# First modulation in two halves, and other orders of work in the first stage

## The chip, the cores and the metric

The kernel is one layer of a hybrid block and runs on one core of one Trainium2 chip. The core's engines are TensorE (PE; its weight loads are PEld), VectorE (DVE, in the code V), ScalarE (ACT, in the code S) and GpSimd (POOL, in the code G); SyncE (SP) issues most DMA loads. The metric is the device time in microseconds of one execution; a kernel's time is the median of its runs.

## The reference

The layer has two parts. The first makes a modulation from a conditioning vector, normalises and modulates 512 latent and 256 context tokens of width 1024, projects them, mixes one half by a two-dimensional DFT and the other by two gated linear recurrences (forward and backward), and projects back. The second retrieves 16 of 16384 experts per head and token.

```python
mod_x = silu(c) @ w_mod + b_mod          # six vectors of 1024: sh1, sc1, g1, sh2, sc2, g2
mod_c = silu(c_ctx) @ w_mod + b_mod      # of these only sh1, sc1 matter
hx = rmsnorm(x, norm1_g) * (1 + sc1_x) + sh1_x
hc = rmsnorm(ctx, norm1_g) * (1 + sc1_c) + sh1_c
fx, ux, gx = split(hx @ w_in);  uc = (hc @ w_in)[u columns]
ux, uc = dwconv(ux), dwconv(uc)
for d, rev in ((0, False), (1, True)):   # r, i: sigmoid gates of the convolved u
    a = exp(-8 * r * softplus(-lam))     # decay
    h = scan(a, sqrt(1 - a * a) * i * u) # context first, then latent
rx = (h_forward + h_backward) * gelu(gx)
x = x + g1 * (concat(rmsnorm(fourier_mix(fx)), rmsnorm(rx)) @ w_out)
h2 = rmsnorm(x, norm2_g) * (1 + sc2) + sh2
x = x + g2 * peer_ffn(h2);  out = rmsnorm(x, final_norm_g)
```

## The kernel before

Everything lies transposed: 128 partitions hold 128 channels, the free axis holds tokens (256 of the context, `C`, then 512 latent, `T`), and eight tiles `d` make the width of 1024. Products in high precision are three matmuls each (`mm3`, lines 131 to 134): every operand is split in a high part (ACT copies it, line 70) and a low part (V, or G where the call says so, subtracts, line 123); `split_w` does this for 1024 columns of a weight.

Weights come in 1 MB blocks through `load` (line 115) into rotating buffers of the pool `raws`: two of the tag `raw`, two of `rawU`. A load waits until a buffer of its tag is free. The loads up to `graw` (`wgate`) are issued by SP in the order of the code (`in_order(first_load, ...)`); later ones where the framework's planner puts them. PE, ACT and V run the first stage in the order of the code, in two stretches that `in_order(start, ...)` fixes; POOL's order is the planner's.

The modulation is 24 blocks of `w_mod`, eight for each third. `mod_mm(n)` (line 217) multiplies block `n` by the conditioning; `mod_out(m)` copies the sum, transposes it with four small matmuls (line 225) and adds the bias (line 229). The first third gives shift and scale of the first norm, for latent and context (`mods`, `modc`). The order of the first stage is: sums of squares of `x` (line 247) and its reciprocal root (`rsqrt`, lines 151 to 154), blocks 0 to 2, sums of squares of the context, blocks 3 to 7, `mod_out(0)`, `A1` (the scale, line 262). Then for each `d` come `hx_norm` (V multiplies by scale and root, line 267; ACT adds the shift and rounds to the high part), `hx_low` (V makes the low part, line 272) and `u_mm`, the projection to the first half of `u`, with the two splits of `wu0` and the decay rates (`decay_rates`, 26 small operations on V, lines 294 to 309) in between.

The second stretch starts with `u_evac` and `conv` and goes on in the order written out in the middle of the code: `gates(k)` (two directions, two gates, each with one context and one latent product into one of five PSUM buffers, freed by ACT's sigmoid), `decays` (lines 396, 397), `scans` (lines 404 to 413; the sum of the two directions is line 413), `gate_branch`, the Fourier products `f_mm`, the DFT over positions `dft_seq` and over channels `dft_head`, `rec_out`, and the output projection `out_mm` in eight parts, each followed by `out_add`. `mod_cols(w)` issues one more block of the modulation and multiplies the one before. The second norm's sums of squares are `x2_sums`; `rstd2` is its root. Then `h2` (lines 705 to 707) and the routing loop over eight heads, whose query weights `wq` are split with the low part on G.

Of the kernel before, what the change touches and what calls it, by code (L numbers as in the profile page):

```python
# [51 lines left out]
def build(tc, xT, ctxT, c2t, vecs, wm, wu, wf, wg, wgate, wo, wq, keys, u, v, urow, vrow,  # L52
# [158 lines left out]
    def mod_mm(n):  # L211
        m, d = n // 8, n % 8
        if d == 0:
            modp[m] = pst("pm")
        t = rawm.pop(n)
        for j in range(4):
            PE.matmul(modp[m][32 * j:32 * j + 32], cc32[:, d], t[:, j * 512:(j + 1) * 512],  # L217
                      start=(d == 0), stop=(d == ND - 1))

    def mod_out(m):  # L220
        sb = bt(F32, 512)
        act(sb, modp[m], AF.Copy)
# [4 lines left out]
        for z, mm in enumerate((mods, modc)[:2 if m == 0 else 1]):
            sl = slice(16 * m, 16 * m + 16)
            V.tensor_tensor(mm[:, sl].rearrange("p (j b) -> p j b", j=4), pv[:, z],
                            vec[:, V_BMOD + 16 * m:V_BMOD + 16 * m + 16].rearrange("p (j b) -> p j b", j=4), op=ALU.add)  # L230
# [52 lines left out]
    hx_norm(0)  # L283
    wpu = [split_w(rawu[0], 0)]
    hx_norm(1)
    hx_low(0)
    wpu.append(split_w(rawu[0], 1))
    hx_norm(2)
    hx_low(1)
    u_mm(pss0, wpu, 0)  # L290
    u_mm(pss0, wpu, 1)

    def decay_rates():
        V.tensor_scalar(s_, e_, 2.0, None, op0=ALU.add)
        V.reciprocal(s_, s_)
        V.tensor_tensor(s_, s_, e_, op=ALU.mult)
        V.tensor_tensor(q_, s_, s_, op=ALU.mult)
        V.memset(sp, 1.0 / 17)
        yield
        for n in (15, 13, 11, 9, 7, 5, 3, 1):  # L300
            V.tensor_tensor(sp, sp, q_, op=ALU.mult)
            V.tensor_scalar(sp, sp, 1.0 / n, None, op0=ALU.add)
            if n in (11, 5):
                yield
        V.tensor_tensor(sp, sp, s_, op=ALU.mult)
        V.tensor_scalar(e_, lam, -1.0, 0.0, op0=ALU.mult, op1=ALU.max)
        V.scalar_tensor_tensor(sp, sp, 2.0, e_, op0=ALU.mult, op1=ALU.add)
        V.tensor_scalar(z8, sp, 8.0, None, op0=ALU.mult)
        V.tensor_scalar(n8, sp, -8.0, None, op0=ALU.mult)

    decay = decay_rates()
    for d in range(3, ND):
        hx_norm(d)
        hx_low(d - 1)
        next(decay, None)
        u_mm(pss0, wpu, d - 1)
    hx_low(ND - 1)
    u_mm(pss0, wpu, ND - 1)
    for _ in decay:
        pass  # L320
# [78 lines left out]
    def scans(ks):  # L399
        for k in ks:  # L400
            for dr in range(2):
# [6 lines left out]
                else:  # L408
# [865 lines left out]
```

## Time and profile before

| | before |
|---|---|
| median of 3 runs | 1479.88 us (1477.38 to 1479.92) |
| profiled execution | 1475.7 us, its span 1473.9 us |
| PE busy | 1390.8 us (94%) |
| DVE busy | 1234.7 us (84%) |
| ACT busy | 614.4 us (42%) |
| POOL busy | 689.6 us (47%) |
| mean granted TensorE clock | 0.973 |
| DMA | 420.61 MB, mean 285 GB/s |

The profile is one execution. Busy time is an average over stages with different limits; the first stage, up to about 270 us, is where the change lies. In a timeline each row has start and length in microseconds, the engine, the line, the operation, what it writes and reads with the shape, the number of merged instructions, and in brackets how long the engine had been idle before it and what ended that. The granted clock is a share of 2.4 GHz: 1.00 is that, 0.50 is 1.2 GHz.

### The profile page before, as it was taken

The numbers are of one execution on the slowest core, as the hardware profiler recorded it, in microseconds if no ns is written. First come the engines' busy times: TensorE is split into PE (matmuls) and PEld (weight loads), VectorE is DVE, ScalarE is ACT, GpSimd is POOL, SyncE is SP. The second block draws the span as 40 slices with busy tenths as digits, with TensorE's granted clock in tenths as the row PEclk, the third lists the DMA queues.
The fourth block names the chain that finished last, engine by engine and source line by source line (L and its number), as shares of the span: only waits on it lengthen the run. The fifth ranks groups of instructions, "written<-read, shape, count | busy, mean of one in ns | idle before, by whom it ended". The sixth has DMA issues, their size and how long they took to land.

```text
span 1473.9 us, 22547 instructions
## 1 busy us (share of the span) xinstructions
PE 1390.8 (94%) x8561; PEld 1285.8 (87%) x8561; DVE 1234.7 (84%) x2178; ACT 614.4 (42%) x880; POOL 689.6 (47%) x466
## 2 busy tenths in 40 slices
PE   5798888999989999999999999998999999899995
PEld 2676655888878999999999999998999999899995
DVE  2867874699987999388989898998898999999973
ACT  3468642534333556443333433333343343343341
POOL 0035255466430000255767656675675765645412
PEclk9899999999999999999999999999999999999998
DMA  9324347232225999999999998999999999999911
GB/s 369 125 80 177 143 172 259 90 128 84 90 77 173 317 305 300 366 342 374 371 367 405 356 409 331 400 369 376 393 378 389 385 375 405 411 415 415 394 45 57
DMA packets 130189, 420.61 MB, mean 285 GB/s; under 512 B 10400, under 2 KB 59808, under 8 KB 106016
## 3 DMA queue, kind: packets, MB, share of 16 engines
q1 hardware_dynamic: 83520, 251.03, 45.7%
q0 software_dynamic: 46560, 168.14, 29.6%
q8 instruction: 67, 1.10, 0.3%
q14 instruction: 42, 0.34, 0.1%
HBM read 385.41 MB, written 33.69 MB: 284 GB/s over the span
## 4 chain that ended last, share of the span: by engine, by line
PE 57%; DVE 12%; DMA 11%; issue 9%; POOL 6%; ACT 3%; SPq 0%; DVEq 0%; POOLq 0%; ACTq 0%
PE ps_ps L132 8%; PE ps_ps L133 8%; PE ps_ps L134 8%; PE ps_pa L132 8%; PE ps_pa L133 8%; PE ps_pa L134 8%; POOL row L1065 6%; DMA row<-vrow,eidx 4%; DMA row<-urow,eidx 4%; DVE wlo L123 2%; DVE oacc L1086 1%; ACT b L70 1%; PE ps_pm L217 1%; ACT whi L70 1%; DVE row L1072 1%
## 5 line engine op out<-in xcount | busy, mean ns | idle before, releaser
L70 ACT ACTIVATE whi<-raw 128x1024 fp32r<-128x1024 f32 x296 | 312.6, 1059 | 602.0 <-PE ps_pa L133 296.8
L123 DVE TENSOR_TENSOR wlo<-raw,whi 128x1024 fp32r<-128x1024 f32 x264 | 328.3, 1246 | 48.3 <-ACT whi L70 46.5
L132 PE MATMUL ps_pa<-h2h,whi 128*128 128x352 f32 x1024 | 336.6, 329 | 4.9 <-ACT act L70 4.9
L133 PE MATMUL ps_pa<-h2l,whi 128*128 128x352 f32 x1024 | 336.0, 328 | 0.0
L134 PE MATMUL ps_pa<-h2h,wlo 128*128 128x352 f32 x1024 | 335.8, 328 | 0.2 <-DVE wlo L123 0.2
L1065 POOL DMA_INDIRECT row<-vrow,eidx x128 | 191.4, 1495 | 133.0 <-DVE oacc L1086 96.7
L1065 POOL DMA_INDIRECT row<-urow,eidx x128 | 198.3, 1549 | 113.2 <-DVE row L1072 57.5
L133 PE MATMUL ps_ps<-wl,whi 128*128 128x352 f32 x640 | 206.8, 323 | 0.0
L134 PE MATMUL ps_ps<-wh,wlo 128*128 128x352 f32 x640 | 206.6, 323 | 0.0
L132 PE MATMUL ps_ps<-wh,whi 128*128 128x352 f32 x640 | 206.4, 323 | 0.0
L132 PEld LDWEIGHTS ps_pa<-h2h,whi 128*128 128x128 f32 x1024 | 195.1, 191 | 6.9 <-ACT act L70 5.6
L134 PEld LDWEIGHTS ps_pa<-h2h,wlo 128*128 128x128 f32 x1024 | 194.6, 190 | 1.3 <-DVE wlo L123 0.4
L133 PEld LDWEIGHTS ps_pa<-h2l,whi 128*128 128x128 f32 x1024 | 194.8, 190 | 0.9
L1072 DVE SCALAR_TENSOR_TENSOR row<-row,hrow 128x1024 f32<-128x1024 f32 x128 | 153.8, 1219 | 32.9 <-DMA row<-urow,eidx 32.5
L1086 DVE SCALAR_TENSOR_TENSOR oacc<-row,gw,oacc 128x1024 f32<-128x1024 f32 x127 | 162.5, 1280 | 11.3 <-DMA row<-vrow,eidx 10.6
L134 PEld LDWEIGHTS ps_ps<-wh,wlo 128*128 128x128 f32 x640 | 120.2, 188 | 0.2 <-DVE wlo L123 0.2
L133 PEld LDWEIGHTS ps_ps<-wl,whi 128*128 128x128 f32 x640 | 120.2, 188 | 0.0
L132 PEld LDWEIGHTS ps_ps<-wh,whi 128*128 128x128 f32 x640 | 120.2, 188 | 0.0
L123 POOL TENSOR_TENSOR wlo<-raw,whi 128x1024 fp32r<-128x1024 f32 x32 | 77.2, 2414 | 91.8 <-ACT whi L70 63.9
L133 PE MATMUL ps_pa<-wl,whi 128*128 128x352 f32 x256 | 82.7, 323 | 0.0
L134 PE MATMUL ps_pa<-wh,wlo 128*128 128x352 f32 x256 | 82.6, 323 | 0.0
L132 PE MATMUL ps_pa<-wh,whi 128*128 128x352 f32 x256 | 82.5, 322 | 0.0
(296 smaller groups left out, 2610.3 us busy)
## 6 DMA issues: line engine op xcount, KB each, us to landing
raw<-u SPq DMA_DIRECT2D x64, 1024.0 KB, 7.5
raw<-v SPq DMA_DIRECT2D x64, 1024.0 KB, 7.9
raw<-wm SPq DMA_DIRECT2D x24, 1024.0 KB, 5.9
Gd<-stg SPq DMA_DIRECT2D x22, 1024.0 KB, 7.6
gt<-Gd SPq DMA_DIRECT2D x16, 1408.0 KB, 11.5
raw<-wq SPq DMA_DIRECT2D x8, 1024.0 KB, 5.2
Ad<-act SPq DMA_DIRECT2D x10, 704.0 KB
act<-Ad SPq DMA_DIRECT2D x10, 704.0 KB
```

Of the source, the lines that this page charges most:

```text
L70: return S.activation(o, i, f, **kw)
L123: lo_ins[0] = (lo_eng or V).tensor_tensor(dst[1], src, dst[0].bitcast(F32), op=ALU.subtract).ins
L132: PE.matmul(ps, a[0], b[0], start=start, stop=False)
L133: PE.matmul(ps, a[0], b[1], start=False, stop=False)
L134: PE.matmul(ps, a[1], b[0], start=False, stop=stop)
L217: PE.matmul(modp[m][32 * j:32 * j + 32], cc32[:, d], t[:, j * 512:(j + 1) * 512], start=(d == 0), stop=(d == ND - 1))
L1065: G.indirect_dma_start(out=t, out_offset=None, in_=tab, in_offset=bass.IndirectOffsetOnAxis(ap=e[:, s:s + 1], axis=0))
L1072: ins = V.scalar_tensor_tensor(t, t, 1.0, hr, op0=ALU.mult, op1=ALU.mult, accum_out=dt[:, s:s + 1])
L1086: ins = V.scalar_tensor_tensor(o, t, g[:, s:s + 1], o, op0=ALU.mult, op1=ALU.add)
```

## The change

The first third of the modulation is laid out anew on the host: blocks 0 to 3 hold the columns of the scale, blocks 4 to 7 those of the shift, each block two tiles `d` of 1024 columns. Each half has its own sum (`mod_first`), and the sum over the two tiles is part of the transposes. The scale is applied to all `d` of `x` before the context's squares are summed; the shifts follow after. `wu0` is loaded ahead of blocks 4 to 7, with its two splits between blocks 5 and 6; the decay rates stand right after the root of `x`. The sum of the two scan directions goes from G to V. The second half of the gate weights (`gp[1]`) is split before the first decays; the first two parts of `w_out` are split after the first DFT head, and a modulation block stands before that head. In the output projection the sums of squares follow the second part instead of the first; block 23 and `mod_out(2)` stand in the eighth part, and the query weights of head 0 are loaded and split (on V) within the loop.

```diff
-    for n in range(4, 8):
-        mod_load(n, ("", "U")[n % 2])
-    rawu = {0: load(wu[0], cuts=2)}
+    rawu = {0: load(wu[0], cuts=2)}
+    for n in range(4, 8):
+        mod_load(n, ("U", "")[n % 2])
     def mod_mm(n):
+        t = rawm.pop(n)
+        if n < 8:
+            m, first, final = -1 - n // 4, n % 4 == 0, n % 4 == 3
+            ds = [2 * (n % 4) + j // 2 for j in range(4)]
+        else:
+            m, first, final = n // 8, n % 8 == 0, n % 8 == 7
+            ds = [n % 8] * 4
+        if first:
             modp[m] = pst("pm")
         for j in range(4):
-            PE.matmul(modp[m][32 * j:32 * j + 32], cc32[:, d], t[:, j * 512:(j + 1) * 512],
-                      start=(d == 0), stop=(d == ND - 1))
+            PE.matmul(modp[m][32 * j:32 * j + 32], cc32[:, ds[j]], t[:, j * 512:(j + 1) * 512],
+                      start=first, stop=final)
+    def mod_first(z):
+        sb = bt(F32, 512)
+        act(sb, modp[-1 - z], AF.Copy)
+        pT = pst("pa", 32)
+        for b in range(4):
+            PE.matmul(pT[:, 4 * b:4 * b + 4], sb[:, b * P:(b + 1) * P], vec[:, V_SEL2:V_SEL2 + 4], start=True, stop=True)
+        pv = pT[:, :16].rearrange("p (b j z) -> p z j b", b=4, j=2)
+        o = 8 - 8 * z
+        for k, mm in enumerate((mods, modc)):
+            V.tensor_tensor(mm[:, o:o + 8].rearrange("p (j b) -> p j b", j=2), pv[:, k],
+                            vec[:, V_BMOD + o:V_BMOD + o + 8].rearrange("p (j b) -> p j b", j=2), op=ALU.add)
...
     rsqrt(rstd[:, sx], m[:, sx], ssx, 1024)
-    for n in range(3):
+    V.tensor_scalar(s_, e_, 2.0, None, op0=ALU.add)
+    V.reciprocal(s_, s_)
...
+    V.tensor_scalar(n8, sp, -8.0, None, op0=ALU.mult)
+    for n in range(4):
         mod_mm(n)
-    mean_squares([xn[d][:, sc] for d in range(ND)], C, ssc, range(ND))
-    rsqrt(rstd[:, sc], m[:, sc], ssc, 1024)
-    for n in range(3, 8):
-        mod_mm(n)
-    mod_out(0)
+    mod_first(0)
     A1 = cpool.tile([P, 2, ND], F32, name="A1")
...
+    for d in range(ND):
+        hx_norm(d, 0, x2[d], sx)
+    mean_squares([xn[d][:, sc] for d in range(ND)], C, ssc, range(ND))
+    rsqrt(rstd[:, sc], m[:, sc], ssc, 1024)
+    for d in range(ND):
+        hx_norm(d, 1, xn[d][:, sc], sc)
+    mod_mm(4)
+    mod_mm(5)
+    wpu = [split_w(rawu[0], h) for h in range(2)]
+    mod_mm(6)
+    mod_mm(7)
+    mod_first(1)
...
+    for d in range(ND):
+        hx_high(d)
+        hx_low(d)
+        u_mm(pss0, wpu, d)
...
-                    G.tensor_tensor(hsum[-1][:, C:], hsum[-1][:, C:], r[:, C:], op=ALU.add)
+                    V.tensor_tensor(hsum[-1][:, C:], hsum[-1][:, C:], r[:, C:], op=ALU.add)
...
     y_split(3)
+    gp[1] = split_w(graw, 1)
     decays([0, 1])
     gate_branch(1)
     gate_weights(3)
-    gp[1] = split_w(graw, 1)
     scans([0, 1])
...
     scans([3])
-    wpo = {k: out_weights(k) for k in range(2)}
...
+    mod_cols(7, "U")
     Y0 = dft_head(0, ab0)
-    mod_cols(7, "U")
+    wpo = {k: out_weights(k) for k in range(2)}
     ab0 = dft_seq(2)
...
+    psk = {}
     for k in range(8):
-        pss = out_mm(k, wpo[k], Ys if k < 4 else mr)
-        if k == 0:
+        psk[k] = out_mm(k, wpo[k], Ys if k < 4 else mr)
+        if k == 1:
             ssf, ssr = pst("pa"), pst("pa")
...
-        out_add(k, pss, rF if k < 4 else None)
+            out_add(0, psk[0], rF)
+        if k:
+            out_add(k, psk[k], rF if k < 4 else None)
...
         if k < 7:
             mod_cols(9 + k, "U")
+        if k == 5:
+            raw0 = load(wq[0])
+        if k == 7:
+            mod_mm(23)
+            mod_out(2)
+        if k == 6:
+            wpq = [split_w(raw0, p, V) for p in range(2)]
     x2_sums(3)
     rsqrt(rstd2, bt(F32, 512), ss2[0], 1024)
-    mod_mm(23)
-    mod_out(2)
...
-            wp = split_w(raw, p, G)
+            wp = split_w(raw, p, G) if h else wpq[p]
```

## Rows read from the trace of the kernel before

**Rows 1.** Stretches: length, busy us (x) of PE, PEld, DVE, ACT, POOL, clock, DMA share, GB/s.
```profile
32.80:49.87 17.07, 10.39 (x34) 7.22 (x35) 9.72 (x20) 7.03 (x11) 0.00 (x0) 0.50 0.72 283
...
67.35:112.57 45.22, 44.46 (x232) 35.39 (x230) 31.72 (x43) 27.04 (x40) 15.00 (x8) 1.00 0.25 94
115.57:121.55 5.98, 5.21 (x15) 4.04 (x15) 5.19 (x6) 5.79 (x7) 0.00 (x0) 0.50 0.76 284
122.36:168.76 46.40, 44.97 (x234) 34.49 (x234) 40.44 (x31) 35.33 (x49) 23.16 (x12) 1.00 0.44 161
168.76:186.71 17.95, 13.56 (x97) 10.61 (x96) 11.58 (x19) 6.71 (x16) 6.14 (x4) 0.90 0.39 136
271.08:1473.90 1202.82, 1164.94 (x7471) 1126.10 (x7470) 1057.10 (x1935) 473.96 (x670) 597.48 (x411) 0.98 0.82 308
```
**Rows 2.** Timeline of PE: modulation blocks, transposes, and the start and end of `u_mm`.
```profile
30.64 1.07 PE L217 MATMUL ps_pm<-raw,cc 128*32 128x512 f32 x8 [1.42 <-DMA raw<-wm]
33.13 1.94 PE L217 MATMUL ps_pm<-raw,cc 128*32 128x512 f32 x8 [1.43 <-DMA raw<-wm]
35.79 1.88 PE L225 MATMUL ps_pa<-vec,b 128*128 128x8 f32 x8 [0.72 <-ACT b L70]
41.10 0.58 PE L132 MATMUL ps_ps<-b,whi 128*128 128x256 f32 x1 [3.43 <-ACT whi L70]
...
65.05 0.27 PE L132 MATMUL ps_ps<-b,whi 128*128 128x256 f32 x1
...
67.14 0.28 PE L132 MATMUL ps_ps<-b,whi 128*128 128x256 f32 x1
```
**Rows 3.** Timeline of SP: two issues of loads.
```profile
31.77 0.33 SPq L115 DMA_DIRECT2D raw<-wgate  x1
...
94.86 0.33 SPq L115 DMA_DIRECT2D raw<-wm  x1
```
**Rows 4.** The chain that ended last: start, length, what; a load from issue to use.
```profile
129.63 4.80 DMA raw<-wf
```
**Rows 5.** Timeline of DVE: a norm of 512 columns, a weight split, a decay rate's step.
```profile
42.62 0.74 DVE L267 SCALAR_TENSOR_TENSOR b<-x,A,b 128x512 f32<-128x512 f32 x1
...
45.10 1.22 DVE L123 TENSOR_TENSOR wlo<-raw,whi 128x1024 fp32r<-128x1024 f32 x1 [0.68 <-ACT whi L70]
...
60.54 0.17 DVE L305 TENSOR_TENSOR sp<-sp,s__152 128x8 f32<-128x8 f32 x1
```
**Rows 6.** Timeline of PE at `gates(2)`: its first matmul and the one after the stop.
```profile
115.57 0.58 PE L132 MATMUL ps_ps<-b,whi 128*128 128x256 f32 x1 [3.00 <-ACT whi L70]
...
122.36 0.50 PE L132 MATMUL ps_ps<-b,whi 128*128 128x512 f32 x1 [0.90 <-ACT b L70]
```
**Rows 7.** Timeline of ACT between `decays` and `scans`.
```profile
113.53 1.99 ACT L70 ACTIVATE whi<-raw 128x1024 fp32r<-128x1024 f32 x2
```
**Rows 8.** Timelines of DVE and PE around the Fourier head.
```profile
157.09 3.43 DVE L123 TENSOR_TENSOR wlo<-raw,whi 128x1024 fp32r<-128x1024 f32 x2
...
168.38 3.40 DVE L123 TENSOR_TENSOR wlo<-raw,whi 128x1024 fp32r<-128x1024 f32 x2
...
172.44 0.39 PE L133 MATMUL ps_pa<-b,c_sb 128*128 128x258 f32 x1 [3.68 <-DVE b L123]
```
**Rows 9.** Timelines of PE and DVE in the output projection.
```profile
196.32 1.78 PE L653 MATMUL ps_pa<-b,ones 128*128 128x512 f32 x2 [2.93 <-POOL b L567]
...
204.43 1.40 DVE L628 SCALAR_TENSOR_TENSOR b<-ps_ps,mods,b 128x512 f32<-128x512 f32 x2
...
217.26 3.47 DVE L558 SCALAR_TENSOR_TENSOR b<-b,vec 128x512 fp32r<-128x512 f32 x2
...
219.86 1.06 PE L217 MATMUL ps_pm<-raw,cc 128*32 128x512 f32 x8
```
**Rows 10.** Timelines of ACT and DVE before `h2`.
```profile
248.03 1.99 ACT L70 ACTIVATE whi<-raw 128x1024 fp32r<-128x1024 f32 x2
...
252.09 2.71 DVE L153 TENSOR_TENSOR b<-b,rstd 128x512 f32<-128x512 f32 x1
```

More of the change, by code (lines that the diff above doesn't have):

```diff
@@ L37 @@
 NG = P // JG
-V_BMOD, V_N1, V_N2, V_FN, V_CW, V_CB, V_BA, V_BX, V_LAM, V_FG, V_LG, V_SEL = (
-    0, 48, 56, 64, 72, 88, 92, 100, 108, 116, 120, 124)
-NV = 132
+V_BMOD, V_N1, V_N2, V_FN, V_CW, V_CB, V_BA, V_BX, V_LAM, V_FG, V_LG, V_SEL, V_SEL2 = (
+    0, 48, 56, 64, 72, 88, 92, 100, 108, 116, 120, 124, 132)
+NV = 136
 NBUF = 35
@@ L226, in mod_out @@
         pv = pT.rearrange("p (b j z) -> p z j b", b=4, j=4)
[L227 to L230, printed above, removed]
+        sl = slice(16 * m, 16 * m + 16)
+        V.tensor_tensor(mods[:, sl].rearrange("p (j b) -> p j b", j=4), pv[:, 0],
+                        vec[:, V_BMOD + 16 * m:V_BMOD + 16 * m + 16].rearrange("p (j b) -> p j b", j=4), op=ALU.add)
     hx = []
@@ L252, in build @@
     rsqrt(rstd[:, sx], m[:, sx], ssx, 1024)
-    for n in range(3):
-        mod_mm(n)
-    mean_squares([xn[d][:, sc] for d in range(ND)], C, ssc, range(ND))
-    rsqrt(rstd[:, sc], m[:, sc], ssc, 1024)
-    for n in range(3, 8):
-        mod_mm(n)
-    mod_out(0)
+    V.tensor_scalar(s_, e_, 2.0, None, op0=ALU.add)
+    V.reciprocal(s_, s_)
+    V.tensor_tensor(s_, s_, e_, op=ALU.mult)
+    V.tensor_tensor(q_, s_, s_, op=ALU.mult)
+    V.memset(sp, 1.0 / 17)
+    for n in (15, 13, 11, 9, 7, 5, 3, 1):
+        V.tensor_tensor(sp, sp, q_, op=ALU.mult)
+        V.tensor_scalar(sp, sp, 1.0 / n, None, op0=ALU.add)
+    V.tensor_tensor(sp, sp, s_, op=ALU.mult)
+    V.tensor_scalar(e_, lam, -1.0, 0.0, op0=ALU.mult, op1=ALU.max)
+    V.scalar_tensor_tensor(sp, sp, 2.0, e_, op0=ALU.mult, op1=ALU.add)
+    V.tensor_scalar(z8, sp, 8.0, None, op0=ALU.mult)
+    V.tensor_scalar(n8, sp, -8.0, None, op0=ALU.mult)
+    for n in range(4):
+        mod_mm(n)
+    mod_first(0)
     A1 = cpool.tile([P, 2, ND], F32, name="A1")
@@ L262, in build, with hx_norm, hx_high @@
         V.scalar_tensor_tensor(A1[:, z], mm[:, 8:16], 1.0, vec[:, V_N1:V_N1 + 8], op0=ALU.add, op1=ALU.mult)
-    def hx_norm(d):
+    def hx_norm(d, z, src, sl):
+        V.scalar_tensor_tensor(xn[d][:, sl], src, A1[:, z, d:d + 1], rstd[:, sl], op0=ALU.mult, op1=ALU.mult)
+    for d in range(ND):
[10 more added lines that the diff above has]
+    mod_first(1)
+    parts = ((sc, modc), (sx, mods))
+    def hx_high(d):
         hx.append(bt2(L))
-        for z, src, sl, mm in ((1, xn[d][:, sc], sc, modc), (0, x2[d], sx, mods)):
-            V.scalar_tensor_tensor(xn[d][:, sl], src, A1[:, z, d:d + 1], rstd[:, sl], op0=ALU.mult, op1=ALU.mult)
+        for sl, mm in parts:
             act(hx[d][0][:, sl], xn[d][:, sl], AF.Identity, bias=mm[:, d:d + 1])
     def hx_low(d):
-        for sl, mm in ((sc, modc), (sx, mods)):
+        for sl, mm in parts:
             V.scalar_tensor_tensor(hx[d][1][:, sl], xn[d][:, sl], mm[:, d:d + 1], hx[d][0][:, sl].bitcast(F32),
@@ L281, in u_mm @@
             mm3(pss[h][1], a, cut(hx[d], slice(C, L)), d == 0, d == ND - 1)
[L283 to L320, printed above, removed]
+    for d in range(ND):
+        hx_high(d)
+        hx_low(d)
+        u_mm(pss0, wpu, d)
     wpu1 = [split_w(rawu[1], h, V, "U") for h in range(2)]
@@ L809, in build @@
     for h in range(8):
-        raw = load(wq[h])
+        raw = load(wq[h]) if h else None
         kraw = qp.tile([P, 256], F32, tag="kraw", name="kraw")
@@ L1203, in prep @@
         i["fourier_out_g"][0], i["lru_out_g"][0])]
-                               + [np.eye(P, dtype=np.float32).reshape(P, 4, 32)[:, :, :2].reshape(P, 8)], 1)
+                               + [np.eye(P, dtype=np.float32).reshape(P, 4, 32)[:, :, :2].reshape(P, 8)]
+                               + [np.eye(P, dtype=np.float32).reshape(P, 2, 2, 32)[..., :2].sum(1).reshape(P, 4)], 1)
     a["c2t"] = np.stack([i["c"][0], i["c_ctx"]]).reshape(2, ND, P).transpose(2, 1, 0)
-    a["wm"] = i["w_mod"][0].reshape(ND, P, 3, 2048).transpose(2, 0, 1, 3)
+    wm = np.array(i["w_mod"][0].reshape(ND, P, 3, 2048).transpose(2, 0, 1, 3))
+    wm[0] = (i["w_mod"][0][:, :2048].reshape(4, 2, P, 2, 1024)[:, :, :, ::-1]
+             .transpose(3, 0, 2, 1, 4).reshape(ND, P, 2048))
+    a["wm"] = wm
     w = i["w_in"][0]
```

3 lines of the change are left out of this document (removed).

## The prediction, made before the run

> **What bounds the kernel now.** The table by stretches comes first [rows 1]: from 271.08 us to the end PE has 1164.9 of 1202.8 us busy, and nothing there is edited, so a shift at 271 is carried to the end one for one. The edits lie before it. Next the PE timeline, for its bracketed idle times: PE loses time at five places, at the first modulation (33 to 44 us), at the gates (112.6 to 122.4), at the Fourier head (168.8 to 172.4), before the sums of squares (193.4 to 196.3) and before `h2` [rows 2, 6, 8, 9, 10]. The wait behind each is what the change must move; the timelines of V (VectorE), ACT and SP give its length.
>
> **First modulation.** Before, the eighth `wm` block is multiplied at 33.13, the transposes run at 35.79, the first product of `u_mm` stands at 41.10 [rows 2], and PE is at the lower clock level (0.50) from 32.80 to 49.87 [rows 1]. `u_mm` ends at 67.1, where the next product's first matmul stands [rows 2].
>
> After, the scales come from the first four blocks, so V's sixteen norms, the context's four root steps (0.74 each at most) and two weight splits (1.22) [rows 5] need not wait for the shifts. Blocks come 2.49 apart (30.64, 33.13 [rows 2]); from the fourth to the eighth are five such steps, the context's 1 MB being one, so the fourth is there at 20.7. One block 1.06, a copy 0.65, transposes 1.0 at full speed, four small operations 0.5: 24.0. V then has 14.8 + 2.4, done by 41.2 at the latest. The decay rates, 26 operations of 0.17 [rows 5] that stood between the products, now lie in V's idle time before the fourth block lands; if they overran it, they would eat into the slack that V has until the shifts.
>
> What is late next is the last block. `wu0` is now loaded ahead of blocks 4 to 7, so these come one step later: block 6 (the seventh) at 33.1, and block 7 needs a buffer of its tag. If it takes the one that block 5 frees (multiplied at 30.64 to 31.7), SP issues it at 31.8 to 32.2, as it issues `wgate` now [rows 3]. A 1 MB load took 4.80 to its first use [rows 4]: 36.6 to 37. SP is in order, so `wu1`, `wgate` and `wg` stand behind it; none is used before `u_mm` ends. Then, at the lower level, one block 1.94, a copy 0.65, transposes 1.88 [rows 2], V 0.3: the shifts stand at 41.6, and `u_mm` starts at 42.3 with its weights split. It no longer waits for V: per `d` a high and a low part of `hx` cost ACT and V some 1.25 each, against 2.09 on PE (65.05 to 67.14 [rows 2]). Full-speed length 8 x 2.09 = 16.7. PE has been idle, so it starts at the lower level, which lasted 3.6 (clock 0.90 over 17.95), 6.0 and 17.1 in three stretches [rows 1]. I take 5, nearest the 6.0 that followed a like wait; half of it, 2.5, is lost. End: 42.3 + 0.4 + 16.7 + 2.5 = 62 to 62.5. **Gain 4.6** (3.5 to 6). From 67.35 to 112.57 PE is busy 44.5 of 45.2 [rows 1], so it arrives whole at the gates.
>
> **The gates.** `gp[1]` is split before the decays. PE now waits 3.00 for it, does 15 matmuls at the lower level (5.98 at 0.50 [rows 1]) and waits 0.90 more, until ACT's sigmoid frees PSUM at 122.36 [rows 6]. The edit moves one of ACT's two copies at 113.53 [rows 7] ahead of the decays, which then start one copy (1.0) later, so square roots and sigmoid stay where they are: PE does its 15 matmuls sooner and waits some 7 us for the same sigmoid. Worse, the lower level, which costs nothing while it covers those 15, then covers the gates behind the wait, and from 122.36 PE is busy 44.97 of 46.40 [rows 1]. **Loss 2.5**, half of 5; at worst 3.4, at best a gain of 3.6, if ACT takes the copy in a pause and the sigmoid comes sooner. The page "TensorE: Matmul & The Clock Gate" of the Trainium skill, in "HAM oscillation — how this bites in real kernels", says that a PE left waiting between bursts starts each burst at half rate; the 0.50 behind the 3.00 wait agrees, so by the rule too this edit costs time.
>
> **Scan sums on V.** Four adds of 0.6 go from POOL to V. While POOL adds, V's two splits take 3.43 [rows 8] instead of 2.4, so V wins back 1.0 of each. About 0; at worst -0.6, at best +0.4 for each of the two adds that V is late for.
>
> **Fourier head.** At 168.38 V does two splits of `w_out` (3.40) before the low part of the first DFT, and PE waits 3.68 for that [rows 8]. The splits now follow the head, and a `wm` block (1.06) fills part of the wait. Of the 17.95 from 168.76 PE is busy 13.56 at clock 0.90 [rows 1]: 3.6 at the lower level, so 11.8 at full speed. New short waits (the head's PSUM freed behind V's `rec_out`; the moved splits ahead of the third DFT's) I put at 1.6, between 0 and the 3.40 moved. 17.95 - 11.8 - 1.6: gain 4.6 at the output projection.
>
> **Output projection.** The sums of squares follow the second product, so a block and a product (1.06 + 5.6) fill the 2.93 wait for POOL. The sums start at 193.4 - 4.6 + 6.7 = 195.5, now at full speed: 0.9 each, not 1.78 [rows 9]. The third product then needs the PSUM that `out_add(0)` frees, 7.1 after the first sum (198.1 to 204.43 + 0.74 [rows 9]); PE has 0.9 + 1.06 + 2.8 to do and stands for 2.3. Behind that V is the bound: from the first sum to the last `rec_norm` at 220.7 [rows 9] its chain takes 22.6, and the fifth product reads its end. It starts at 196.4 and has one split (1.2) less: 217.8. The fifth product stands at 220.9 (219.86 + 1.06 [rows 9]) and needs that end three groups of 0.7 on, at 223.0. **Gain 5.2**, the head's 4.6 included (0 to 7.5).
>
> **Before `h2`.** The query weights' splits leave ACT (1.99 at 248.03, just ahead of `rstd`) and POOL (beside which V took 2.71 for 0.7 at 252.09) [rows 10] for the seventh product, where both engines have room. But the last `wm` block, its copy and its transposes now stand before the sums' last matmuls: 1.0 + 0.65 + 1.1 on the path, less 0.7 that ACT's copies already delayed `rstd`. 2.0 + 0.9 - 2.1: **gain 0.8** (-0.5 to 2.9).
>
> Sum: 4.6 - 2.5 + 0 + 5.2 + 0.8 = 8.1; I take 8. The profiled execution lasted 1475.7 (span 1473.9, 1.8 around it): 1467.7 after. The median is 1479.88, 4.2 above it; by that scale 1471.9.
>
> **Rivals.** (a) Block 7 gets the buffer of `wu0` and waits for V's last split, by 41: it lands 4 to 5 later, and the first gain falls from 4.6 to 0.5: 1476.0. For: `wu0` precedes it in its tag. Against: at 94.86 a `wm` load starts as the block before it is done [rows 3], while `wgate`, older in that tag, is not split until 113.53 [rows 7]: the first buffer freed is taken. 0.13. (b) The gates gain 3.6 instead of losing 2.5: 1465.8. For: ACT pauses in the decays; against: the pause is V's and POOL's, and comes later with them. 0.10. (c) POOL puts the four additions of the first two products ahead of the multiplications of `rec_norm`; V's chain ends 5 later and takes back the whole 5.2: 1477.1. For: they come first in the code; against: `r` is ready before them. 0.12. (d) Slower: PE stays at the lower level from the wait at the gates through gates, gate branch and Fourier product. Each us of it costs half; with the 2.5 counted already it decides from 21 us on (half of 21 is 8 + 2.5). Kept to the third Fourier product, 27 us, it gives 1482.9. For: the gates free PSUM piece by piece, with short waits; against: the longest such stretch, 17.07, had waits up to 3.43 in it [rows 1, 2]. 0.07. [...] (e) The gain is made and lost again in the routing, where V and PE are both full: 1479.9. 0.08.
>
> **Numbers.** Forecast 0.50, its own range 1469 to 1474.5. A measurement of this kernel tells 0.2%, 3 us, from no change. Faster holds the forecast, (b), most of (a) and half of (c): 0.79; the same 0.13; slower 0.08. The range goes from 1465 (b) to 1478.5 (past c).
>
> **What would show it.** The eighth block multiplied near 36.8 and `u_mm` ending at 62 to 63; an idle time of about 7 inside the gates and the lower level behind it; no wait of 3.68 at the head; one of 2.3 in the third product; the 2.71 back at 0.7. Wrong if the eighth block lands after 40, if the sigmoid comes over 1 us sooner after the first gate branch, or if the fifth product still starts at 220.

## The result and the profile after

| | before | after |
|---|---|---|
| median | 1479.35 us (1475.81 to 1487.45, 14 runs) | 1472.01 us (1465.42 to 1475.31, 14 runs) |
| ratio | | 0.9936, 95% interval 0.9919 to 0.9953 |
| profiled execution, span | 1475.7, 1473.9 | 1473.89, 1472.1 |

The changed kernel is faster by 0.5 to 0.8%; 1471.9 was forecast. The two spans differ by 1.8 us only, but from `h2`'s first matmul to the end the first profiles take 1216.1 us before (1473.9 - 257.8) and 1220.3 after (1472.1 - 251.76), in code that is the same but for the head 0 query weights. So the terms are read from positions ahead of `h2`. A position is where a modulation block (8, 10, 13, 20: the `mod_mm` of that number) or `h2` starts on PE. "Second profile" is a later execution of the same kernel (r1, r3 below).

| start on PE, us | before | second | after | second | gain, mean of both | predicted |
|---|---|---|---|---|---|---|
| block 8 (behind `u_mm`) | 93.73 | 95.05 | 90.34 | 89.61 | 4.4 | 4.6 |
| block 8 to 10 (gates) | 34.77 | 36.35 | 36.90 | 36.86 | -1.3 | -2.5 |
| block 10 to 20 (scans, head, output projection) | 98.02 | 97.85 | 93.00 | 93.02 | 4.9 | 5.2 |
| block 20 to `h2` | 31.27 | 31.45 | 31.51 | 33.10 | -0.9 | 0.8 |
| `h2`'s first matmul | 257.80 | 260.70 | 251.76 | 252.59 | 7.1 | 8 |

The stretches of the changed kernel, as in [rows 1]; length, busy us (x) of PE, PEld, DVE, ACT, POOL, clock, DMA share, GB/s:

```profile
21.30:31.54 10.24, 9.54 (x31) 6.60 (x24) 7.53 (x24) 3.04 (x9) 0.00 (x0) 0.50 1.00 356
38.37:48.60 10.23, 7.32 (x27) 4.81 (x28) 5.32 (x11) 4.67 (x10) 0.00 (x0) 0.50 0.79 313
116.87:123.70 6.83, 4.72 (x14) 4.04 (x15) 6.69 (x7) 5.83 (x11) 2.20 (x2) 0.50 0.11 47
...
265.67:1472.10 1206.43, 1164.10 (x7471) 1124.87 (x7470) 1056.71 (x1935) 474.15 (x670) 600.51 (x411) 0.98 0.81 307
```

Before, one stretch of 17.07 us at the lower level covered the transposes and the start of `u_mm`. After, there are two of 10.2, and the first lies where no stage was meant to suffer: over the fourth block, the first transposes and the context's sums of squares.

PE in the first stage (start, length, operation, idle before), to be held against [rows 2]:

```profile
25.41 6.72 PE L265 MATMUL ps_ps<-b,ones 128*128 128x256 f32 x16
32.06 1.92 PE L223 MATMUL ps_pm<-raw,cc 128*32 128x512 f32 x16
35.00 1.06 PE L223 MATMUL ps_pm<-raw,cc 128*32 128x512 f32 x8 [1.02 <-DMA raw<-wm]
39.69 1.94 PE L223 MATMUL ps_pm<-raw,cc 128*32 128x512 f32 x8 [3.62 <-DMA raw<-wm]
42.34 1.87 PE L232 MATMUL ps_pa<-vec,b 128*128 128x4 f32 x8 [0.72 <-ACT b L70]
45.09 0.58 PE L132 MATMUL ps_ps<-b,whi 128*128 128x256 f32 x1 [0.87 <-ACT b L70]
...
63.77 0.28 PE L132 MATMUL ps_ps<-b,whi 128*128 128x256 f32 x1
```

The sums take 6.72 us; blocks 4 and 5 (the 16 matmuls of 32.06) stand behind them. SP, first row, sends block 7's load right as block 5 ends (33.98); V, second fence, had its weight splits done at 40.05:

```profile
34.05 0.33 SPq L115 DMA_DIRECT2D raw<-wm  x1
```
```profile
37.69 2.36 DVE L123 TENSOR_TENSOR wlo<-raw,whi 128x1024 fp32r<-128x1024 f32 x2
...
172.76 3.84 DVE L123 TENSOR_TENSOR wlo<-raw,whi 128x1024 fp32r<-128x1024 f32 x2 [0.19 <-ACT whi L70]
...
248.15 0.69 DVE L153 TENSOR_TENSOR b<-b,rstd 128x512 f32<-128x512 f32 x1
```

The sums do not hold block 5 in every execution. In e2 (below), whose first stage has the same code, they took 3.70 us, and PE then stood waiting for block 5's own load (first fence, PE); SP sent block 7's load as that block ended (second):

```profile
31.91 1.06 PE L223 MATMUL ps_pm<-raw,cc 128*32 128x512 f32 x8 [1.34 <-DMA raw<-wm]
```
```profile
33.03 0.33 SPq L115 DMA_DIRECT2D raw<-wm  x1
```

PE at the gates, the head, the output projection and `h2`, for [rows 6, 8, 9]:

```profile
118.98 0.79 PE L132 MATMUL ps_ps<-b,whi 128*128 128x512 f32 x1 [7.34 <-ACT b L70]
...
167.84 0.39 PE L133 MATMUL ps_pa<-b,c_sb 128*128 128x258 f32 x1 [0.88 <-DVE b L123]
...
195.31 1.02 PE L667 MATMUL ps_pa<-b,ones 128*128 128x512 f32 x2
...
203.46 0.50 PE L132 MATMUL ps_ps<-b,whi 128*128 128x512 f32 x1 [2.33 <-DVE b L641]
...
242.21 1.06 PE L244 MATMUL ps_pa<-vec,b 128*128 128x8 f32 x8 [0.89 <-ACT b L70]
...
251.76 1.22 PE L132 MATMUL ps_ps<-h2h,whi 128*128 128x512 f32 x2 [5.82 <-ACT h2h L70]
```

The 3.00 and 0.90 of [rows 6] have become one wait of 7.34; the 3.68 of [rows 8] is 0.88, because the two splits of `w_out` now start at 172.76, behind the head; the sums wait for nothing (2.93 in [rows 9]), and the third product waits 2.33. ACT ahead of `h2`, for [rows 10]: the two copies of 1.99 us are still there, now of the next weights `u`, and they wait for their load with the copy of block 23's sum behind them:

```profile
118.45 3.33 ACT L70 ACTIVATE b<-ps_ps,vec 128x256 f32<-128x256 f32 x7
...
239.67 2.00 ACT L70 ACTIVATE whi<-raw 128x1024 fp32r<-128x1024 f32 x2 [4.49 <-DMA raw<-u]
241.58 0.58 ACT L70 ACTIVATE b<-ps_pm 128x512 f32<-128x512 f32 x1
...
245.98 0.69 ACT L70 ACTIVATE rstd<-ps_pa,epst 128x512 f32<-128x512 f32 x1 [2.79 <-PE ps_pa L655]
```

(The row of 118.45 is the gates' sigmoid, that of 245.98 the root of the second norm.)

### The profile page after: what moved, and what is told of

It is laid out like the page before. It is cut to its first block, busy times and chain, and to the rows that moved or that the text cites. A ratio compares the mean times of both kernels' runs of the same rounds, so it can differ in the third digit from the quotient of the medians.

```text
span 1472.1 us, 22568 instructions
## 1 busy us (share of the span) xinstructions
PE 1390.7 (94%) x8569; PEld 1287.3 (87%) x8569; DVE 1235.5 (84%) x2186; ACT 613.4 (42%) x881; POOL 680.6 (46%) x460
## 5 line engine op out<-in xcount | busy, mean ns | idle before, releaser
L1086 POOL DMA_INDIRECT row<-vrow,eidx x128 | 196.2, 1533 | 131.6 <-DVE oacc L1107 93.5
L123 POOL TENSOR_TENSOR wlo<-raw,whi 128x1024 fp32r<-128x1024 f32 x30 | 72.0, 2402 | 84.8 <-ACT whi L70 56.9
```

The costliest lines, as they stand in the source:

```text
L123: lo_ins[0] = (lo_eng or V).tensor_tensor(dst[1], src, dst[0].bitcast(F32), op=ALU.subtract).ins
L1086: G.indirect_dma_start(out=t, out_offset=None, in_=tab, in_offset=bass.IndirectOffsetOnAxis(ap=e[:, s:s + 1], axis=0))
```

## The experiments

Each of e2 to e7 and e9 is the changed kernel with one edit, e1 and e8 undo several; positions are read as above, in one profile each. The runs e1 to e4 shared one chip (before there: 1482.33), e5 to e8 another (1481.8), r1 and r2 a third (1482.87).

| | median, us | ratio to before (95%) | block 8 | 8 to 10 | 10 to 20 | 20 to `h2` | `h2` |
|---|---|---|---|---|---|---|---|
| e1 first modulation only | 1475.26 | 0.9945 (0.9923 to 0.9967) | 89.87 | 34.77 | 98.00 | 31.27 | 253.92 |
| e2 gate split late | 1471.89 | 0.9931 (0.9907 to 0.9955) | 87.69 | 34.76 | 95.02 | 31.40 | 248.87 |
| e3 shift blocks first | 1470.57 | 0.9914 (0.9892 to 0.9937) | 87.50 | 37.76 | 93.06 | 31.33 | 249.65 |
| e4 block 23 after sums | 1470.20 | 0.9913 (0.9886 to 0.9940) | 90.47 | 37.72 | 92.99 | 30.00 | 251.18 |
| e5 sums after first | 1475.25 | 0.9952 (0.9940 to 0.9965) | 88.45 | 36.84 | 94.74 | 31.53 | 251.56 |
| e6 scan sums on POOL | 1472.50 | 0.9935 (0.9918 to 0.9951) | 89.31 | 37.28 | 92.84 | 34.14 | 253.57 |
| e7 head order of before | 1475.22 | 0.9957 (0.9944 to 0.9970) | 90.42 | 37.18 | 96.00 | 31.36 | 254.97 |
| e8 three undone | 1466.78 | 0.9899 (0.9877 to 0.9920) | 87.52 | 34.78 | 95.76 | 29.47 | 247.52 |
| r1 changed, again | 1472.89 | 0.9939 (0.9908 to 0.9969) | 89.61 | 36.86 | 93.02 | 33.10 | 252.59 |
| r2 three undone, again | 1467.58 | 0.9904 (0.9876 to 0.9931) | 88.71 | 34.76 | 95.09 | 29.46 | 248.01 |

Intervals of 4 to 6 us do not tell apart parts of 2 us; the positions do.

**e1: the first modulation alone.** Everything else is as before (the lines on the query weights of head 0 are left out here):

```diff
-                    V.tensor_tensor(hsum[-1][:, C:], hsum[-1][:, C:], r[:, C:], op=ALU.add)
+                    G.tensor_tensor(hsum[-1][:, C:], hsum[-1][:, C:], r[:, C:], op=ALU.add)
...
-    gp[1] = split_w(graw, 1)
     decays([0, 1])
     gate_branch(1)
     gate_weights(3)
+    gp[1] = split_w(graw, 1)
...
     scans([3])
+    wpo = {k: out_weights(k) for k in range(2)}
...
+    Y0 = dft_head(0, ab0)
     mod_cols(7, "U")
-    Y0 = dft_head(0, ab0)
-    wpo = {k: out_weights(k) for k in range(2)}
...
-        if k == 1:
+        if k == 0:
...
-        if k == 7:
-            mod_mm(23)
-            mod_out(2)
...
+    mod_mm(23)
+    mod_out(2)
```

> The changed kernel with everything behind the first modulation put back (gate split, scan sums, Fourier head, output projection, query weights as before). Theory: the first modulation alone is worth what block 8 shows, 3.4 us (90.34 after, 93.73 before); so block 8 within 1 us of 90.3, the eighth block multiplied between 36.5 and 40, block 23 and the first matmul of h2 3.4 us (2.5 to 4.5) earlier than before (249.2, 257.8), and the time 3.4 us under the kernel before, ratio 0.9977. Rival: nearly all of the gain comes from the Fourier head and the output projection, and the shift at block 8 is the luck of one profile: block 8 within 1 us of 93.7 and a ratio of 1.000.

Block 8 stands at 89.87 and from there every distance is that of the first profile of before (34.77, 98.00, 31.27): the part stands by itself, and it reaches `h2` whole, 3.9 us against that profile. The time does not tell its size: the ratio of 0.9945 is further from 1 than the 0.9977 expected, which lies outside the interval; against the second profile of before `h2` stands 6.8 us ahead, 0.5%, which lies inside. The waits of before come back with the other edits undone (PE at the gates):

```profile
111.71 0.58 PE L132 MATMUL ps_ps<-b,whi 128*128 128x256 f32 x1 [3.00 <-ACT whi L70]
```

**e2: the second half of the gate weights split late, as before.**

```diff
-    gp[1] = split_w(graw, 1)
     decays([0, 1])
     gate_branch(1)
     gate_weights(3)
+    gp[1] = split_w(graw, 1)
     scans([0, 1])
```

> The changed kernel with gp[1] split behind gate_weights(3) again. Theory: the early split only lengthens the wait at the gates; put back, the long wait of 7.3 us falls apart into 3.0, 0.7 and 0.9, the sigmoid stands where it did (21.3 us after the end of the first gate branch), the lower clock level lies in the 15 matmuls in front of it, and block 10 comes 1.7 to 2.5 us sooner against block 8 than after (36.9 after, 34.8 before): 34.5 to 35.2. Time 2 us under the changed kernel, 1470. Rival: the early split is a gain; block 10 then comes later against block 8, by 0.5 to 3.6 us.

PE at the gates (first fence), and the stretches at the lower level, there and in the third output product (second; columns as in [rows 1]):

```profile
109.53 0.39 PE L132 MATMUL ps_ps<-b,whi 128*128 128x256 f32 x1 [3.00 <-ACT whi L70]
...
116.32 0.50 PE L132 MATMUL ps_ps<-b,whi 128*128 128x512 f32 x1 [1.33 <-ACT b L70]
```
```profile
110.90:114.31 3.41, 3.31 (x10) 2.83 (x11) 2.65 (x3) 3.41 (x5) 0.00 (x0) 0.50 0.89 324
...
199.65:203.06 3.41, 3.41 (x8) 2.74 (x9) 3.41 (x5) 1.45 (x2) 3.41 (x3) 0.50 0.00 0
```

At its place the edit costs about what was forecast: 2.1 us are back (34.76 against 36.90), the lower level lying over matmuls that have time. But they are not kept. Block 13 comes 1.0 later behind block 10 (20.22 against 19.26, with a wait of 0.67 for a weight's low part at 131.80), and the third output product, behind its wait of 2.32, ran at the lower level (199.65), as it did not in the changed kernel. This is not one profile's chance: e8 and r2, which also split late, show both (20.23 and 20.26 behind block 10; the lower level from 201.01 and 201.73), and none of the seven profiles with the early split and the same wait (after, r1, e3, e4, e6, e7, e9) does. What ties the one to the other was not found. From block 8 to 20 it is 129.78 here and 129.90 there: the early split of `gp[1]` is, over the stage, worth nothing either way.

**e3: `wu0` loaded behind blocks 4 to 7, its splits behind the shifts.**

```diff
-    rawu = {0: load(wu[0], cuts=2)}
     for n in range(4, 8):
-        mod_load(n, ("U", "")[n % 2])
+        mod_load(n, ("", "U")[n % 2])
+    rawu = {0: load(wu[0], cuts=2)}
...
     mod_first(1)
+    wpu = [split_w(rawu[0], h) for h in range(2)]
```

> The changed kernel with wu0 loaded behind blocks 4 to 7 again (tags as before) and split behind the shifts. Theory: block 7 is late only because SP holds its load until block 5 has freed the buffer, behind the context's sums; without wu0 in the tag it is multiplied at 33 to 36 instead of 39.69. Then the splits of wu0 on V, which follow the norms, end last: u_mm runs from 41.5 instead of 45.1, and block 8 comes 3 to 5 us sooner than after, at 85.3 to 87.5. Time 4 us under the changed kernel, 1468. Rival: V's norms and splits were the bound all along and the late block hides behind them: block 8 within 1 us of 90.3.

PE, block 7 and the start of `u_mm` (first fence), and ACT's first copy of `wu0` (second):

```profile
34.18 1.07 PE L223 MATMUL ps_pm<-raw,cc 128*32 128x512 f32 x8 [0.38 <-DMA raw<-wm]
...
40.15 0.58 PE L132 MATMUL ps_ps<-b,whi 128*128 128x256 f32 x1 [3.13 <-ACT b L70]
```
```profile
37.40 1.06 ACT L70 ACTIVATE whi<-raw 128x1024 fp32r<-128x1024 f32 x1 [1.49 <-DMA raw<-wu]
```

Block 7 comes at 34.18 instead of 39.69. The edit takes two things away at once, the wait for a buffer and the 1 MB of `wu0` ahead of it; as blocks land some 2.5 apart, an estimate gives 2.5 of the 5.5 us to the second and 3 to the first, so "only" in the expectation goes too far. The wait moves behind the transposes (3.13: ACT adds the first shift behind its copies of `wu0`, which wait for their load), and `u_mm` starts 4.9 earlier than in the changed kernel. Of that 2.8 is left at block 8, just under the 3 expected, since `u_mm` lies at the lower level to about 47.3. Block 8 stands at 87.50; the same edit inside e8 and r2 gave 87.52 and 88.71. The mean of these, 87.9, is 1.6 ahead of the mean of the eight profiles with the changed first stage (89.5).

**e4: block 23 multiplied behind the sums of squares, as before.**

```diff
-        if k == 7:
-            mod_mm(23)
-            mod_out(2)
...
     rsqrt(rstd2, bt(F32, 512), ss2[0], 1024)
+    mod_mm(23)
+    mod_out(2)
```

> The changed kernel with block 23 and mod_out(2) behind the last sums and the root again; the query weights of head 0 stay early. Theory: the last block, its copy and its transposes hold the sums' last matmuls back by 2.8 us and eat what the query weights gave; put back, the first matmul of h2 comes 1 to 2.9 us sooner against block 22 than after (18.2 after, 17.9 before): 15.3 to 17.2; the lower end if POOL's split of the u weights does not meet V's root steps. Time 2 us under the changed kernel. Rival: the root waits for A2 and for ACT's copies whatever stands on PE: 18 within 0.5.

PE, the sums' last matmuls and the first on `h2`:

```profile
243.69 1.12 PE L655 MATMUL ps_pa<-b,ones 128*128 128x512 f32 x2 [0.72 <-ACT b L70]
...
251.18 1.22 PE L132 MATMUL ps_ps<-h2h,whi 128*128 128x512 f32 x2 [3.53 <-ACT h2h L70]
```

From block 20 to `h2` it takes 30.00 instead of 31.51, and the wait at `h2` falls from 5.82 to 3.53. The move of block 23 takes 1.5 us, the rest of that edit (the query weights) gives 1.3 against before (31.27).

**e5: the sums of squares behind the first product, as before.**

```diff
-        if k == 1:
+        if k == 0:
             ssf, ssr = pst("pa"), pst("pa")
...
-            out_add(0, psk[0], rF)
-        if k:
-            out_add(k, psk[k], rF if k < 4 else None)
+        out_add(k, psk[k], rF if k < 4 else None)
```

> The sums of squares go back behind the first product of the output projection; all else is as changed. Theory (two waits traded: 2.9 for POOL ahead of the sums against 2.3 in the third product): the wait ahead of the sums is back at 2.5 to 3.2 with sums at the lower level behind it, the wait of 2.33 in the third product is gone, and block 20 stands 74.2 to 76.4 us behind block 13 (73.75 in the changed kernel, 78.36 before). Rival 1 (the place of the sums is worth nothing, since V's chain sets the end): 73.4 to 74.1. Rival 2 (the sums' place is what gave the output projection's gain): 77.5 or more. Time: within 0.2% of the changed kernel by the theory.

PE at the sums (first fence) and the stretch behind the wait (second):

```profile
189.77 1.94 PE L667 MATMUL ps_pa<-b,ones 128*128 128x512 f32 x2 [2.90 <-POOL b L579]
```
```profile
189.94:193.36 3.42, 3.42 (x7) 0.89 (x7) 0.86 (x2) 0.69 (x1) 0.00 (x0) 0.50 0.04 14
```

The wait is back with the lower level behind it, the 2.33 is gone, and block 20 stands 75.45 us behind block 13 (73.75 in the changed kernel): this place of the sums is worth 1.7.

**e6: the scan sums on POOL, as before.**

```diff
-                    V.tensor_tensor(hsum[-1][:, C:], hsum[-1][:, C:], r[:, C:], op=ALU.add)
+                    G.tensor_tensor(hsum[-1][:, C:], hsum[-1][:, C:], r[:, C:], op=ALU.add)
```

> The four additions of the scans' sums go back from V to POOL; all else is as changed. Theory (V wins beside an idle POOL what it pays for the additions, 1.0 against 1.2): block 20 stands 73.2 to 74.4 us behind block 13 (73.75 in the changed kernel) and no new wait of PE over 1 us appears before the output projection. Rival (V's four additions of 0.6 are on the path): block 20 comes 1.2 to 2.4 sooner. Rival (POOL's additions slow V's splits on the path): 1 to 2 later. Time: within 0.2% of the changed kernel.

V (first fence) and POOL (second):

```profile
154.80 3.44 DVE L123 TENSOR_TENSOR wlo<-raw,whi 128x1024 fp32r<-128x1024 f32 x2
```
```profile
155.03 2.12 POOL L426 TENSOR_TENSOR b<-b 128x512 f32<-128x512 f32 x1 [8.51 <-DVE b L424]
166.33 1.28 POOL L426 TENSOR_TENSOR b<-b 128x512 f32<-128x512 f32 x1 [9.18 <-DVE b L424]
```

73.55 from block 13 to 20, 0.2 from the changed kernel: nothing, as forecast. Two splits take 3.44 us beside POOL's addition and 2.36 without (in the row of 37.69 above). The Trainium skill's page "SBUF — State Buffer", section "SBUF: two separate sides", says that V with two SBUF inputs and a GpSimd operation that reads SBUF lock each other out for a whole instruction. The trace agrees: POOL's addition takes 2.12 beside the splits (155.03), which read both inputs from SBUF, and 1.28 beside operations of V that read one of them from PSUM (166.33), and V loses 1.08.

**e7: the splits of `w_out` ahead of the Fourier head, the block behind it, as before.**

```diff
     scans([3])
+    wpo = {k: out_weights(k) for k in range(2)}
...
-    mod_cols(7, "U")
     Y0 = dft_head(0, ab0)
-    wpo = {k: out_weights(k) for k in range(2)}
+    mod_cols(7, "U")
```

> The two splits of the output weights go back ahead of the Fourier head, and the modulation block behind it; all else is as changed. Theory (4.6 of the gain are this order: the wait of 3.7 and the lower level behind it): a wait of 3.4 to 3.8 stands behind the head's matmuls, the granted clock falls to 0.50 there for 3 to 6 us, and block 20 stands 77.0 to 78.4 us behind block 13 (73.75 in the changed kernel, 78.36 before). Rival (V's chain in the output projection hides the wait): 73.7 to 75.5. Time: 2 to 6 us over the changed kernel.

PE at the head (first fence) and the stretch behind the wait (second):

```profile
170.46 0.58 PE L133 MATMUL ps_pa<-b,c_sb 128*128 128x258 f32 x1 [3.00 <-DVE b L123]
```
```profile
168.75:175.57 6.82, 5.11 (x21) 3.23 (x22) 5.41 (x9) 2.78 (x6) 2.55 (x2) 0.50 0.51 171
```

The wait (3.00, where 3.4 to 3.8 was expected, and 1.08 ahead of it) and the lower level are back. Block 20 stands 76.75 behind block 13, just under the 77.0 expected: the order is worth 3.0, not 4.6. With the 1.7 of e5 the two make 4.7, and from block 13 to 20 the changed kernel gains 4.6 (78.36 - 73.75).

**e8: three edits undone together (e2, e3 and e4).**

> Three edits at once: the second half of the gate weights is split late again, the 1 MB of weights loaded ahead of the last four modulation blocks goes behind them (and its splits behind the shifts), and block 23 is multiplied behind the sums of squares. Theory (each part stands by itself and is carried to the next by a full PE): first matmul on h2 at 251.76 - 2.1 - 2.8 - 1.5 = 245.4, between 243.5 and 247; by the time, 1464 to 1468 where the changed kernel has 1471 to 1472. Rival 1 (the gains overlap: what PE wins early it waits for V in the output projection): 248 to 250.5. Rival 2 (won ahead of h2 and lost in the routing): 245.4 at h2 and a time of 1470 or more.

PE, block 23's transposes and the first matmul on `h2`:

```profile
242.92 1.06 PE L244 MATMUL ps_pa<-vec,b 128*128 128x8 f32 x8 [0.78 <-ACT b L70]
...
247.52 1.22 PE L132 MATMUL ps_ps<-h2h,whi 128*128 128x512 f32 x2 [3.54 <-ACT h2h L70]
```

`h2` starts at 247.52, half a us past the range of the theory. Against the changed kernel: 2.8 at block 8, 2.0 behind block 20, and -0.6 between, since the 2.1 of the gates is given back as in e2. The median, 1466.78, is that of the theory.

**r1 and r2: the changed kernel and e8's version again, on one chip.**

> The changed kernel once more, on the chip that also runs the version with three parts undone. What is open: block 8 stood at 87.7 to 90.5 us in seven profiles with the same code ahead of it, and the lower clock level fell in other places there. Theory (the place of the lower level among the context's sums and the first blocks differs between executions, and with it block 5's end, block 7's load and the end of u_mm): block 7 comes 5 to 6 us behind block 5's end unless a wait for its own load is shorter, block 8 between 87.5 and 90.7; where the context's sums run at full speed (3.7 us), block 8 stands under 89. Rival (block 8 is fixed at 90.4 by the code of the changed kernel alone): 90.2 to 90.6. Time 1469 to 1475.

> The version with three parts undone once more, beside the changed kernel on the same chip. Theory (4 to 6 us ahead at h2 are carried to the end): 3 to 7 us under the changed kernel on this chip, intervals of the two ratios to before that do not overlap or hardly. Rival (the first median was luck of the late, row-driven part, which differs by several us between profiles): within 2 us of the changed kernel.

The difference is 5.3 us (1472.89 and 1467.58), within the 3 to 7 expected, though the intervals of the two ratios still overlap. Block 8 came at 89.61, so it is not fixed; but the sums' speed alone does not set it: in e7 they ran at full speed (3.70) and block 8 stood at 90.42, since a lower level from 32.21 to 49.28 followed. r1 showed one more thing, ahead of `h2`; ACT first, then PE:

```profile
240.51 2.00 ACT L70 ACTIVATE whi<-raw 128x1024 fp32r<-128x1024 f32 x2 [6.09 <-DMA raw<-u]
242.42 0.58 ACT L70 ACTIVATE b<-ps_pm 128x512 f32<-128x512 f32 x1
```
```profile
243.05 1.06 PE L244 MATMUL ps_pa<-vec,b 128*128 128x8 f32 x8 [2.49 <-ACT b L70]
```

The load of `u` took 6.56 us from its issue (233.95) to ACT's first copy, 4.96 in the first profile (234.71 to 239.67). ACT works in order, so block 23's copy waited for it, and PE 2.49 instead of 0.89.

**r3: the kernel before, a second profile; e9: blocks 4 and 5 ahead of the context's sums.** One run each, on a fourth chip: 1484.83 and 1480.62 us. The kernel before ran there once more, at 1474.19, 10.6 under r3 with the same code, so these single times tell nothing and only positions are read.

```diff
+    mod_mm(4)
+    mod_mm(5)
     mean_squares([xn[d][:, sc] for d in range(ND)], C, ssc, range(ND))
...
-    mod_mm(4)
-    mod_mm(5)
```

> The kernel before once more, for a second profile. What is open: the changed kernel's two profiles stand 6.0 and 5.2 us ahead at h2's first matmul, while the two medians differ by 7 and 10 us. Theory 1 (the first stage of the kernel before is as its one profile shows, and the rest is the late part, which differs between executions): block 8 at 93.0 to 94.5, h2's first matmul at 257.0 to 258.6. Theory 2 (the one profile of before was an early one in the first stage too, as its execution of 1475.7 us stands 4 us under the median): h2's first matmul at 259 or later.

> Blocks 4 and 5 are multiplied ahead of the context's sums of squares, which stand behind them in the changed kernel; nothing else is changed. Theory (block 7's load is issued when block 5 has been multiplied, and V's work for the context has some slack): block 5 at 31.7 to 32.2 whatever the clock level is, block 7 at 37.6 to 38.2, the sums at 33 to 37, V's last split at 44 to 47 instead of 40.05, so that u_mm waits for V and starts at 45 to 48, later than 42.4 to 45.1 in the profiles of the changed first stage. Rival (V has slack enough): u_mm starts at 42.3 to 43.4, and block 8 stands at 87.5 to 88.6.

r3 bears out theory 2: `h2` at 260.70, 2.9 later than in the first profile of before, 1.3 of it at block 8 and 1.6 at the gates, where the lower level lasted longer than the 5.98 us of [rows 1]:

```profile
116.93:127.17 10.24, 8.66 (x25) 6.92 (x26) 9.38 (x9) 9.35 (x14) 2.35 (x2) 0.50 0.54 205
```

In e9 block 7's load goes out at 34.05 again: with the sums out of the way block 5 still starts at 32.41 only, behind a wait of 0.45 for its own load, and runs to 33.98 in part at the lower level. Block 7 is multiplied at 38.79, past the 38.2 expected. The sums stand at 33.91, and V (first fence) and `u_mm` (second, PE) are late as the theory had it:

```profile
43.19 2.36 DVE L123 TENSOR_TENSOR wlo<-raw,whi 128x1024 fp32r<-128x1024 f32 x2
```
```profile
33.91 3.72 PE L265 MATMUL ps_ps<-b,ones 128*128 128x256 f32 x16
...
46.29 0.58 PE L132 MATMUL ps_ps<-b,whi 128*128 128x256 f32 x1 [4.66 <-ACT b L70]
```

So V has less slack there than it would need, and the sums stand rightly ahead of blocks 4 and 5: block 8 stands at 91.88. From block 20 to `h2` it took 35.88, the longest of all.

## Why the prediction was right, and where it was not

**The sum.** 8 was forecast, 7.1 is the difference of the two pairs of profiles at `h2`, 7.3 that of the medians. That the median came within 0.2 us of the forecast is luck: the four parts of the table missed by 0.2 to 1.7, not all the same way. Of the scale from the profiled execution to the median (4.2), r3 shows why it was needed: the first profile of before was an early one, 2.9 at `h2` and 6.3 behind it (1216.1 against 1483.1 - 260.70 = 1222.4).

**First modulation (4.6; 3.4 in the first pair, 4.9 as the mean of 8 profiles against 2).** The mechanism held: block 7 got the buffer that block 5 frees, so rival (a) is out (34.05, not 41). The step that failed is the issue "at 31.8 to 32.2" and with it "36.6 to 37": the working took over 30.64 as the start of block 5. In six of the eight profiles with this first stage PE waited 0.42 to 1.34 for block 5's own load and started it at 31.91 to 32.55; in the other two (the changed kernel and r1) PE had the sums and block 4 ahead of it without a break. The issue came at 33.03 to 34.27, block 7, 4.75 to 5.64 later for the 4.80 of the working, at 37.85 to 39.69, `u_mm` at 42.37 to 45.09 instead of 42.3. Why block 5's load landed 1.3 to 1.9 later than worked out is not shown. In the changed kernel `u_mm` started 2.8 late and gave back 0.9: it took 18.7 (to 63.77) instead of 19.6, as 3.5 us of it (to 48.60), not 5, lay at the lower level. The terms of its end, 42.3 + 0.4 + 16.7 + 2.5, make 61.9; the 4.6 was taken from 62.5. That the size fits is luck in part: against the one profile it was worked out on, the eight gain 4.2.

**The gates (-2.5).** The wait of "some 7" was 7.34, the sigmoid stayed where it was (the matmul that it releases stands 28.64 behind block 8, at 118.98, and stood 28.63 behind it before, at 122.36), and the lower level fell behind it: 2.1 lost at that place, and rival (b) is out. The -1.3 of the table has r3 in it: block 10 stands 36.84 to 37.76 behind block 8 in all eight profiles with the early split, and 34.76 to 34.78 in five of the six with the late one, 36.35 in r3. What the prediction did not see is that this loss is made good later (e2), and that the old order can lose there too (1.6 in r3).

**Scan sums (0).** Right by e6, with the two prices it named: 1.08 per pair of splits, four additions of 0.69 for its 0.6.

**Head and output projection (5.2).** 4.9, but divided otherwise than "the head's 4.6 included" said: 3.0 for the head's order (e7), 1.7 for the sums' place (e5). The third product's wait was 2.33, as worked out, and behind it V sets the pace; rival (c), POOL's additions first, did not happen.

**Before `h2` (0.8).** Wrong in sign: -0.2 in the first pair. Two of the three terms came: from ACT's root to the first norm it took 4.14 (245.98 to 250.12) instead of 6.24 (249.92 to 256.16), for the 2.0, as the 2.71 fell to 0.69; and from V's last addition to `x` (its end) to ACT's root 4.80 (241.18 to 245.98) against 2.75 in e4 (242.11 to 244.86), for the 2.1 of the block's place (e4 gains only 1.5 of it at `h2`, as the root and what follows took 4.67 there). The term that failed is the 0.9, for which the working shows no row: without the block, that stretch is 2.75 and was 2.46 before (247.46 to 249.92). The step "the query weights' splits leave ACT" left ACT empty in the working, and the planner put the copies of the next weights, `u`, in the same place; in the changed kernel they wait for a load, and block 23's copy waits for them. How long they wait differs: from block 20 to `h2` it is 31.33 to 31.53 in five of the eight profiles with this order, but 33.10 in r1, 34.14 in e6 and 35.88 in e9, where the transposes waited 2.49, 1.84 and 1.92; in e6 and e9 the last sums also ran at the lower level, two in 2.05 and 2.06 instead of 1.10.

**Rivals (d) and (e).** The lower level behind the gates ended at 123.70 and none followed before 249.99. What the routing does to the gain can't be read from single profiles: from `h2` to the end they last 1216.1 to 1226.8 in the three with head 0's query weights as before (before, r3, e1; mean 1221.8) and 1216.5 to 1225.3 in the eleven with them changed (mean 1220.4). Neither these means nor the medians, which differ by as much as the positions at `h2`, show a loss. (That "nothing there is edited" from 271 us on is not quite so: these weights are.)

**What stays open.** Which execution gets its lower level where, and why the third output product has it with the late split only: the causes were not found. A version with e3 and e4 but the gates as changed was not run; e2 lets one expect that it comes out as e8's did.

## What to carry to other kernels

A load that waits for a buffer is issued when the instruction that frees it has run: whatever delays that instruction, its own data, work ahead of it or the clock level, delays the load. A landing time read before an edit does not hold behind it. When work is taken off an in-order engine, ask what the planner puts in its place, and put nothing short and urgent behind a copy that waits for a load. Undo an edit and read positions a stage further on, too: 2.1 us won at the gates were gone some 80 us later.

## What the runs showed of the hardware

- The same code shows the lower clock level in other places from execution to execution: the context's sums took 3.70 to 6.72 us in the eight profiles with the changed first stage, with no edit near them.
- The same wait of 2.32 to 2.33 in the third output product was followed by the lower level in all three profiles with the late split of `gp[1]` (e2, e8, r2) and in none of the seven with the early one, though the edit lies some 80 us ahead.
- In the changed kernel the level was down from 116.87, during the wait that ended at 118.98, so a part of the low stretch fell on idle time. The Trainium skill's page "TensorE: Matmul & The Clock Gate", section "HAM oscillation — how this bites in real kernels", tells of bursts that start at half rate behind a wait; the rows at 118.98 (7.34) and 189.77 (2.90) agree, the 2.33 of the changed kernel at 203.46 shows a shorter wait without it.
- A load of 1 MB of `u` took 4.96 and 6.56 us from issue to use at the same place in two executions.
